# Mixer of a Fourier and FFN layer: four w_mod sums on GpSimd and ScalarE, splits and norm steps in another order

## The chip, the cores and the metric

The kernel runs on one core of one Trainium2 chip. TensorE does matrix products into PSUM, VectorE (DVE in the rows) and ScalarE (ACT) elementwise work, GpSimd (POOL) elementwise work in SBUF and some DMA issues, SyncE (SP) the other DMA issues. The metric is device time in microseconds (us) of one execution, smaller is better.

## The reference, cut to what matters

One layer (`DEPTH = 1`, so mixer 0) on 1024 tokens of width 1024, all in fp32:

```python
sh1, sc1, gt1, sh2, sc2, gt2 = ada_params(c, w_mod[i], b_mod[i])   # silu(c) @ w_mod + b_mod, six rows of 1024
a_lat = modulate(h_lat, g_norm_mix[i], sh1, sc1)                   # rms_norm(h, g) * (1 + scale) + shift
y_lat = fourier_mix(a_lat, w_fnet_out[j])                          # real part of a 2-D FFT, 4 groups of 256, then @ w_out
h_lat = h_lat + gt1 * y_lat
h_lat = h_lat + gt2 * conv_ffn(modulate(h_lat, g_norm_ffn[i], sh2, sc2), ...)
return rms_norm(h_lat, g_final)
```

`conv_ffn` is an up-projection to 2 x 2816 columns, a depthwise convolution over three tokens, silu times value, and a down-projection.

## The kernel before, in words

Products of fp32 are made of three reduced products: each operand is split into a high part (a cast on ScalarE) and a low part (a subtraction on VectorE). Such subtractions are called lows here.

**Stages.** The mixer takes the first 160 us or so. Two transforms (products with cosine and sine tables, lines 290 to 313 and 405 to 452) give the tiles `ph, pl, qh, ql` of four groups g, and the Nyquist row `p1`. Then `fnet_block(0)` multiplies them with the output weights `W` for the even tokens and `fnet_block(1)` for the odd ones, each in eight tiles dt of 128 channels; one dt is 25 matmuls (13 into `pw`, 12 into `qw`). ScalarE and VectorE put them into `ha`, GpSimd issues a DMA that adds x to it (line 555). Then each tile is squared (ScalarE, line 471), the squares are added (line 476), TensorE sums them over channels (`rstd_col`, tile `ssps`), VectorE and GpSimd make the inverse root (`r`, with a power on GpSimd), VectorE spreads it on a diagonal, and TensorE broadcasts it (`rb`). `norm2` multiplies by it and gives the operands of the FFN. The FFN begins with plain products `c<chunk><row><block>` (`plain`), and goes on in a seven-product scheme (X, Y, Z, then dX, dY), which is most of the run.

**w_mod.** The rows of `mods` are sums over a tile of w_mod (128 x 1024) times silu(c), one tile (s, n) for each of eight columns n: s = 2 is the gate gt1, 4 the FFN scale, 3 the FFN shift. `mod_sum` (line 145) does product and sum in one VectorE instruction; its second operand `silp` lies in PSUM. `silc` holds the same in SBUF. Each sum lets the next tile load (`wm_ahead`).

**Weights.** `w_prep` loads a unit k of the output weights, GpSimd makes sum and difference, ScalarE the high part; `w_lo(k)` is the low on VectorE, which also starts the load of unit k + 8; `w_last` does the same for the Nyquist weights `wl`.

**What sets the order.** Each engine works its instructions in order. VectorE's and SyncE's order is the order of the code from the start (`manual_schedule`), GpSimd's and ScalarE's from `fnet_block(0)` on, TensorE's from `fnet_block(1)` on; before these places a scheduler sets it. PSUM banks come from a ring of six (`bank`), so a product waits until the sixth tile before it has been read; two more are given by `small`, once `silp` is released (`after_sil`). The list `between` says what VectorE does between the groups of the second transform, `while_even` and `while_odd` what follows each dt, `amid_odd` what TensorE does between `pw` and `qw` of a dt.

## Time and profile before

| what | us |
|---|---|
| median of 3 runs | 825.66 |
| lowest, highest | 824.72, 827.84 |
| the profiled execution, its own time | 826.69 |
| its span, first to last instruction | 824.9 |
| TensorE busy | 778.9 |
| VectorE busy | 606.7 |
| ScalarE busy | 344.4 |
| GpSimd busy | 128.2 |

The rows further down come from the one profiled execution; its times count from the start of the span. "Busy" of TensorE does not say at which clock it ran: the granted clock is a column of its own.

### The profile page before, as it was taken

Reading aid. Unit: us, or ns where it says so; the run is one execution under the profiler, and the core shown is the slowest. Engines: PE = TensorE matmul, PEld = TensorE weight load, DVE = VectorE, ACT = ScalarE, POOL = GpSimd, SP = SyncE. Lnnn points to the kernel's source line nnn. Section 1 sums busy time; section 2 is a strip of 40 time slices with the busy share of each in tenths; the row PEclk is TensorE's granted clock in tenths of the full one; section 3 lists DMA queues with packets and bytes.
Section 4 is the critical chain, followed back from the end, with each engine's and each line's share of the span. In section 5 each row is a group of like instructions: output and inputs, shape, how many; then the busy total and the mean of one; then the engine's idle time right before and its main releaser. Section 6 shows DMA issues by size and latency. Waiting matters only on the chain.

```text
span 824.9 us, 10510 instructions
## 1 busy us (share of the span) xinstructions
PE 778.9 (94%) x3588; PEld 633.3 (77%) x3588; DVE 606.7 (74%) x1001; ACT 344.4 (42%) x617; POOL 128.2 (16%) x168
## 2 busy tenths in 40 slices
PE   1998979799999999999999999999999999999994
PEld 0585978588888888888888888888888888888883
DVE  5998976697867777877777777776747766648573
ACT  7364425425623334343333334433544435345520
POOL 2053431100112121212121121212110000000000
PEclk9999989799999999999999999999999999999995
DMA  9999764702398777858597778676999765655532
GB/s 331 407 335 341 217 178 91 217 27 89 89 288 204 199 192 205 242 142 246 146 254 198 193 221 256 141 195 155 266 294 356 231 191 184 199 183 176 182 149 102
DMA packets 81959, 171.30 MB, mean 208 GB/s; under 512 B 9001, under 2 KB 13865, under 8 KB 81906
## 3 DMA queue, kind: packets, MB, share of 16 engines
q1 hardware_dynamic: 67218, 143.89, 49.6%
q0 software_dynamic: 14688, 26.75, 20.4%
q8 instruction: 28, 0.46, 0.2%
q14 instruction: 25, 0.20, 0.1%
HBM read 130.49 MB, written 51.64 MB: 221 GB/s over the span
## 4 chain that ended last, share of the span: by engine, by line
PE 82%; DVE 9%; DMA 3%; issue 2%; ACT 2%; POOL 1%; POOLq 0%; DVEq 0%; SPq 0%; ACTq 0%
PE Y L693 19%; PE dX L1091 15%; PE X L693 13%; PE Z L693 13%; PE dY L1091 11%; PE c L693 8%; DVE wm L145 2%; DMA ha<-in_xt 2%; DMA wm<-in_wmod 1%; DVE ha L542 1%; PE ssps L1065 1%; DVE ha L572 1%; DVE z L216 1%; PE s2p L441 1%; DVE w L216 1%
## 5 line engine op out<-in xcount | busy, mean ns | idle before, releaser
L616 DVE TENSOR_TENSOR dn<-wd,dn 128x512 fp32r<-128x512 f32 x154 | 99.9, 689 | 69.3 <-ACT dn L612 68.6
L612 ACT CAST dn<-wd 128x512 fp32r<-128x512 f32 x154 | 88.6, 618 | 99.8 <-PE dX L1091 41.5
L1091 PE MATMUL dX<-dn,dn 128*128 128x512 f32 x528 | 123.5, 394 | 0.0
L1091 PEld LDWEIGHTS dX<-dn,dn 128*128 128x128 f32 x528 | 99.1, 188 | 23.2 <-issue 0.5
L755 POOL DMA_DIRECT2D ha<-ha x44 | 38.9, 968 | 348.2 <-DVE ha L696 158.7
L1091 PE MATMUL dY<-dn,dn 128*128 128x512 f32 x396 | 92.1, 394 | 0.0
L1091 PEld LDWEIGHTS dY<-dn,dn 128*128 128x128 f32 x396 | 74.4, 188 | 17.2
L696 DVE TENSOR_TENSOR ha<-Y,ha 128x512 f32<-128x512 f32 x57 | 39.4, 690 | 25.6 <-PE Y L693 25.6
L979 ACT COPY ha<-X 128x512 f32<-128x512 f32 x19 | 11.1, 586 | 110.2 <-PE X L693 110.2
L742 ACT ACTIVATE ha<-ha 128x512 f32<-128x512 f32 x44 | 27.8, 632 | 57.2 <-DVE ha L697 57.2
L145 DVE CUSTOM_DVE_ANT_0 wm<-wm,silp 128x1024 f32<-128x1024 f32 x32 | 37.9, 1213 | 0.4 <-DMA wm<-in_wmod 0.2
L1069 POOL TENSOR_TENSOR r<-r,mhalf 128x4 f32<-128x4 f32 x2 | 2.0, 1020 | 200.6 <-DVE r L1068 200.6
L798 POOL DMA_DIRECT2D sg_s<-in_wdn x22 | 29.9, 1373 | 9.2 <-DMA sg_s<-in_wdn 9.2
L798 POOL DMA_DIRECT2D sg_s<-sg_s x22 | 27.5, 1258 | 16.8 <-DMA sg_s<-sg_s 9.8
L697 DVE SCALAR_TENSOR_TENSOR ha<-ha,vec 128x512 f32<-128x512 f32 (+1 forms) x38 | 28.6, 752 | 1.4
L697 DVE SCALAR_TENSOR_TENSOR ha<-X,vec,ha 128x512 f32<-128x512 f32 (+1 forms) x38 | 28.4, 746 | 0.7
L696 DVE TENSOR_TENSOR ha<-Z,ha 128x512 f32<-128x512 f32 x38 | 26.0, 685 | 1.2 <-PE Z L693 1.2
L166 PE MATMUL gr<-wm,sil 128*32 128x512 f32 x32 | 10.3, 771 | 15.2 <-ACT sil L256 15.1
L696 DVE TENSOR_TENSOR ha<-ha 128x512 f32<-128x512 f32 x33 | 22.4, 685 | 0.0
L771 ACT COPY ha<-ha 128x512 f32<-128x512 f32 x11 | 6.8, 621 | 33.7 <-DVE ha L697 33.7
L166 PEld LDWEIGHTS gr<-wm,sil 128*32 128x32 f32 x32 | 3.1, 131 | 23.0 <-issue 20.6
L555 POOL DMA_DIRECT2D ha<-in_xt x14 | 12.7, 927 | 43.4 <-DVE ha L542 37.5
(947 smaller groups left out, 2000.2 us busy)
## 6 DMA issues: line engine op xcount, KB each, us to landing
wm<-in_wmod SPq DMA_DIRECT2D x40, 512.0 KB, 7.5
ha<-ha POOLq DMA_DIRECT2D x44, 256.0 KB, 5.2
sg_s<-in_wdn SPq DMA_DIRECT2D x44, 256.0 KB, 6.0
wd<-sg_s SPq DMA_DIRECT2D x44, 256.0 KB, 2.7
us_u<-ha SPq DMA_DIRECT2D x33, 256.0 KB, 2.0
wd<-in_wdn SPq DMA_DIRECT2D x33, 256.0 KB, 3.1
wd<-us_u SPq DMA_DIRECT2D x33, 256.0 KB, 3.4
us_T<-ha SPq DMA_DIRECT2D x22, 256.0 KB, 5.2
```

The costliest lines, as they stand in the source:

```text
L145: nc.vector.tensor_tensor_reduce(out=t, in0=t, in1=silp, scale=1.0, scalar=0.0, op0=ALU.mult, op1=ALU.add, accum_out=mods[:, s, n:n + 1])
L166: nc.tensor.matmul(rows[x][32 * j:32 * j + 32, :], lhsT=sil32[:, 4 * q + j, :], rhs=tiles[j][:, 512 * x:512 * x + 512], start=(q == 0), st ...
L216: nc.vector.scalar_tensor_tensor(out=t, in0=xraw[4 * i + f + 1][:, cs_], scalar=rr[:, 4 * i + f + 1:4 * i + f + 2], in1=xraw[4 * i + f][:, ...
L612: nc.scalar.copy(out=t[:, HALF[0]], in_=src)
L616: eng.tensor_tensor(out=t[:, HALF[1]], in0=src, in1=t[:, HALF[0]].bitcast(F32), op=ALU.subtract)
L693: nc.tensor.matmul(ps, lhsT=lh, rhs=rh, start=(first and j == 0 and x == 0), stop=(last and j == 3 and x == 2), skip_group_check=more)
L696: tt = lambda out, a, b, op, eng=nc.vector: eng.tensor_tensor(out=out, in0=a, in1=b, op=op)
L697: stt = lambda out, a, s, b, op0, op1: nc.vector.scalar_tensor_tensor(out=out, in0=a, scalar=s, in1=b, op0=op0, op1=op1)
L742: nc.scalar.activation(out=u[c, blk], in_=u[c, blk], func=AF.Silu)
L755: nc.gpsimd.dma_start(out=t, in_=other, accum_op=ALU.add)
L798: nc.gpsimd.dma_start(out=sg[n][k], in_=sg[a][k] if a[0] == "s" else block(k, a), accum_op=ALU.add, max_dma_last_dim=2048)
L1091: nc.tensor.matmul(BANKS[i][g], lhsT=lh, rhs=rh, start=(i in FIRST and k == 0 and x == 0), stop=(k == K2 - 1 and x == 2), skip_group_check ...
```

## The change

Four w_mod tiles, (4,1), (4,3), (3,2) and (3,4), are no longer summed by VectorE: GpSimd multiplies the tile by `silc` in place (`mod_mul`), and ScalarE adds it up with a copy that accumulates (`mod_acc`). In the second transform the two `p1` steps come ahead of the first weight lows, the lows are dealt out anew over `between`, and three w_mod sums come later in it. The even half's rms chain moves from dt 1 to dt 2 of the odd block; its first norm follows at the end of dt 2 (`late`), the last two w_mod sums of s = 3 stand inside the chain, and `ssps` takes a bank of the ring. Norms and up-projection lows of the first chunk come earlier in the odd block, its squares later. The odd half's chain moves from the first two products of the FFN into the third.

```diff
+    def mod_mul(s, n):
+        t = w_tiles.pop((s, n))
+        nc.gpsimd.tensor_tensor(out=t, in0=t, in1=silc, op=ALU.mult)
+        return s, n, t
+    def mod_acc(s, n, t):
+        nc.scalar.activation(out=t, in_=t, func=AF.Copy, accum_out=mods[:, s, n:n + 1])
+        wm_ahead(1)
...
     mod_tiles(2, 0, 8)
-    mod_tiles(4, 0, 4)
+    for n in (0, 2):
+        m = mod_mul(4, n + 1)
+        mod_tiles(4, n, n + 1)
+        mod_acc(*m)
...
-    w_lo(0, 1, 2, 3)
-    w_last(0)
     for ps, n, c0 in ((l0, 258, 0), (l1, 256, 258)):
...
+    w_lo(0, 1)
...
-    between = [lambda: (w_lo(4, 5), mod_tiles(4, 4, 5)), lambda: (w_lo(6, 7), w_last(1), mod_tiles(4, 5, 6)),
-               lambda: (gate1(), mod_tiles(4, 6, 8)),
-               lambda: (w_lo(8, 9, 10, 11), gate_ffn(), mod_tiles(3, 0, 1))]
+    between = [lambda: (w_lo(2, 3), w_last(0), w_lo(4)), lambda: (mod_tiles(4, 4, 5), w_lo(5, 6, 7), w_last(1)),
+               lambda: (gate1(), mod_tiles(4, 5, 7)),
+               lambda: (mod_tiles(4, 7, 8), w_lo(8, 9, 10, 11), gate_ffn(), mod_tiles(3, 0, 1))]
...
     def while_even(dt):
-        if dt:
-            mod_tiles(3, dt, dt + 1)
-        for d in {2: (0,), 3: (1,), 4: (2,), 5: (3,), 6: (4, 6), 7: (5, 7)}.get(dt, ()):
+        if dt in (1, 3):
+            later.append(mod_mul(3, dt + 1))
+        if dt in (1, 3, 4):
+            mod_tiles(3, {1: 1, 3: 3, 4: 5}[dt], {1: 2, 3: 4, 4: 6}[dt])
+        if dt in (2, 4):
+            mod_acc(*later.pop())
+        for d in {2: (0,), 3: (1,), 4: (2,), 5: (3,), 6: (4,), 7: (6, 5, 7)}.get(dt, ()):
...
     def while_odd(dt):
-        if dt > 2:
-            squares(1, dt - 3)
-            spill(1, dt - 3)
-            stat(1, dt - 3)
-        if dt == 0:
-            mod_bias(3, mods[:, 3, :])
-            after_sil()
-            load_raw(0, "g")
-            load_raw(0, "v")
-        elif 1 < dt < 6:
-            norm2(0, even[1], {2: (1, 2), 3: (3, 4), 4: (5, 6), 5: (7,)}[dt])
-            if dt == 3:
-                for n in ("A11", "A12", "A21", "A22"):
-                    ops[0, n] = op_hi(part(0, n), f"op0{n}")
-        if dt > 5:
-            for n in (("A11", "A12"), ("A21", "A22"))[dt - 6]:
-                op_lo(ops[0, n], part(0, n))
+        if 2 < dt < 6:
+            norm2(0, even[1], {3: (1, 2), 4: (3, 4, 5), 5: (6, 7)}[dt])
+        if dt == 5:
+            for n in ("A11", "A12", "A21", "A22"):
+                ops[0, n] = op_hi(part(0, n), f"op0{n}")
+            op_lo(ops[0, "A11"], part(0, "A11"))
+            op_lo(ops[0, "A12"], part(0, "A12"))
+        if dt > 5:
+            stats_odd(*{6: (0, 1, 2), 7: (3, 4)}[dt])
+        if dt == 7:
+            op_lo(ops[0, "A21"], part(0, "A21"))
+            op_lo(ops[0, "A22"], part(0, "A22"))
     def amid_odd(dt):
-        if dt == 1:
-            even.append(rstd_col(sacc[0], 512))
-            tb.append(stage("tb"))
-            rstd_diag(even[0], 512, tb[0][:, 512:])
-        elif dt == 2:
-            even.append(rstd_row(512, tb[0][:, 512:]))
+        if dt == 2:
+            even.append(rstd_col(sacc[0], 512, bank))
+            after_sil()
+            mod_tiles(3, 6, 7, silc)
+            tb.append(t_tile())
+            rstd_diag(even[0], 512, tb[0])
+            mod_tiles(3, 7, 8, silc)
+            mod_bias(3, mods[:, 3, :])
+            load_raw(0, "g")
+            load_raw(0, "v")
+    def late_odd(dt):
+        if dt == 2:
+            even.append(rstd_row(512, tb[0]))
             norm2(0, even[1], (0,))
...
+    def rms_odd():
+        C["rc"], C["dg"] = rstd_col(sacc[1], 512), t_tile()
+        rstd_diag(C["rc"], 512, C["dg"])
     plain(0, 1, 1, bank)
-    rc = rstd_col(sacc[1], 512)
-    dg1 = t_tile()
-    rstd_diag(rc, 512, dg1)
-    plain(0, 2, 1, bank, lambda: C.update(rb=rstd_row(512, dg1)))
+    plain(0, 2, 1, bank)
...
-    norm2(1, C["rb"], range(2))
...
-    plain(1, 1, 1, bank)
+    plain(1, 1, 1, bank, {("1", 0): rms_odd, ("2", 1): lambda: C.update(rb=rstd_row(512, C["dg"]))})
+    norm2(1, C["rb"], range(2))
```

On VectorE, in the second transform, before: the sums of w_mod tiles (4,2) and (4,3) (`wm_569`, `wm_572`), lows of units 0 to 3, then the `p` steps (`p1`), then the first split.

```order
L145 ISA wm_569,mods<-wm_569,silp 128x1024
...
L145 ISA wm_572,mods<-wm_572,silp 128x1024
...
L366 TENSOR_TENSOR w0l<-u_503,w0h 128x2x256
L366 TENSOR_TENSOR w1l<-u_509,w1h 128x2x256
L366 TENSOR_TENSOR w2l<-u_515,w2h 128x2x256
L366 TENSOR_TENSOR w3l<-u_521,w3h 128x2x256
L382 SCALAR_TENSOR_TENSOR wl<-wlh_666,vec,wlt_551 128x256
L422 SCALAR_TENSOR_TENSOR p_611<-p1h_671,vec,s2l_612 128x258
L422 SCALAR_TENSOR_TENSOR p_611<-p1h_674,vec,s2l_613 128x256
L403 TENSOR_TENSOR pl_599<-s2p_0_677,ph_595 128x258
```

The same place now:

```order
L145 ISA wm_569,mods<-wm_569,silp 128x1024
...
L433 SCALAR_TENSOR_TENSOR p_613<-p1h_640,vec,s2l_614 128x258
L433 SCALAR_TENSOR_TENSOR p_613<-p1h_643,vec,s2l_615 128x256
L376 TENSOR_TENSOR w0l<-u_503,w0h 128x2x256
L376 TENSOR_TENSOR w1l<-u_509,w1h 128x2x256
L416 TENSOR_TENSOR pl_601<-s2p_0_660,ph_597 128x258
```

The `p` steps moved ahead of all lows, and the sum of (4,3) has left VectorE's queue.

On GpSimd, in the even block, before: the DMAs that add x to `ha` and the additions of squares (`sacc`).

```order
L555 DMA ha<-in_xt 128x512 x4
L476 TENSOR_TENSOR sacc_828<-sacc_828,sq 128x512
L555 DMA ha<-in_xt 128x512
L476 TENSOR_TENSOR sacc_828<-sacc_828,sq 128x512
L555 DMA ha<-in_xt 128x512
L476 TENSOR_TENSOR sacc_828<-sacc_828,sq 128x512 x2
L555 DMA ha<-in_xt 128x512
L489 TENSOR_TENSOR r<-r,mhalf 128x4
```

The same place now (`wm_595` is tile (3,2), `wm_769` is (3,4)):

```order
L572 DMA ha<-in_xt 128x512 x2
L158 TENSOR_TENSOR wm_595<-wm_595,silc 128x1024
L572 DMA ha<-in_xt 128x512 x2
L158 TENSOR_TENSOR wm_769<-wm_769,silc 128x1024
L489 TENSOR_TENSOR sacc_830<-sacc_830,sq 128x512
L572 DMA ha<-in_xt 128x512
L489 TENSOR_TENSOR sacc_830<-sacc_830,sq 128x512
L572 DMA ha<-in_xt 128x512
L489 TENSOR_TENSOR sacc_830<-sacc_830,sq 128x512 x2
L572 DMA ha<-in_xt 128x512 x2
L505 TENSOR_TENSOR r<-r,mhalf 128x4
```

Two products came in among the DMAs, and two DMAs instead of one stand ahead of the power for `r`.

On ScalarE, in the second transform, now: the two accumulating copies (`wm_566` is tile (4,1), `wm_572` is (4,3)) among the copies of the first group.

```order
L432 CAST p1h_640<-s2l_614 128x258
L415 CAST ph_597<-s2p_0_660 128x258
L162 ACTIVATE wm_566,mods<-wm_566 128x1024
L415 CAST ph_597<-s2p_0_661 128x256
L432 CAST p1h_643<-s2l_615 128x256
L415 CAST qh_605<-s2q_662 128x512
L162 ACTIVATE wm_572,mods<-wm_572 128x1024
L415 CAST ph_598<-s2p_1_703 128x258
```

The copies were there before, without the two accumulating ones, and the second `p1h` stood behind the first `ph` of the next group.

## Rows read from the trace of the kernel before

**Rows 1.** The page, part 1: busy time of each engine, share, instructions.

```profile
PE 778.9 (94%) x3588; PEld 633.3 (77%) x3588; DVE 606.7 (74%) x1001; ACT 344.4 (42%) x617; POOL 128.2 (16%) x168
```

**Rows 2.** Waits of TensorE, whole span: total us, times, longest.

```profile
PE ssps L485 <- DVE sacc L476: 6.7, 2, 5.1
PE c L693 <- DVE op0A L616: 4.7, 1, 4.7
```

**Rows 3.** Three stretches: busy time of the engines, mean clock, DMA.

```profile
65.00:75.00 10.00, 7.50 (x27) 5.06 (x25) 9.54 (x21) 2.29 (x5) 0.06 (x1) 0.83 1.00 381
115.00:125.00 10.00, 7.64 (x36) 7.35 (x36) 4.97 (x14) 1.94 (x5) 2.82 (x3) 0.66 0.65 186
140.00:165.00 25.00, 17.95 (x72) 13.88 (x71) 16.77 (x33) 10.91 (x21) 3.62 (x4) 0.80 0.68 190
```

**Rows 4.** Timeline, second transform: start, duration (us), instruction, wait before it.

```profile
63.91 1.22 DVE L145 CUSTOM_DVE_ANT_0 wm<-wm,silp 128x1024 f32<-128x1024 f32 x1
...
70.04 0.48 DVE L422 SCALAR_TENSOR_TENSOR p<-p1h,vec,s2l 128x256 fp32r<-128x256 f32 x1 [0.44 <-ACT p1h L421]
...
69.65 2.08 PE L441 MATMUL s2p<-ac,dg 128*128 128x256 f32 x4 [2.50 <-DVE p L422]
```

**Rows 5.** Timeline of ScalarE, first stage: a square with its accumulator.

```profile
8.38 1.04 ACT L196 ACTIVATE junk<-xr 128x1024 f32<-128x1024 f32 x1
9.32 0.19 ACT L196 ACTIVATION_READ_ACCUMULATOR junk<-xr 128x1 f32 x1
```

**Rows 6.** Lines L358, L476 (duration ns least, median, most); two timeline rows.

```profile
L358 POOL TENSOR_TENSOR u<-u x16: 722/738/1174, 49.7 to 86.4; 128x256 f32<-128x256 f32 x16
...
L476 POOL TENSOR_TENSOR sacc<-sacc,sq x4: 1282/1612/1848, 101.5 to 111.2; 128x512 f32<-128x512 f32 x4
...
101.45 1.62 POOL L476 TENSOR_TENSOR sacc<-sacc,sq 128x512 f32<-128x512 f32 x1
...
101.50 2.13 DVE L366 TENSOR_TENSOR w3l<-u,w3h 128x512 fp32r<-128x512 f32 x1
```

**Rows 7.** Timeline: GpSimd on weight unit 8; TensorE at the first Fourier product.

```profile
76.76 1.17 POOL L358 TENSOR_TENSOR u<-u 128x256 f32<-128x256 f32 x1
...
82.58 0.36 PE L533 MATMUL pw<-ph,w0h 128*128 128x258 f32 x1 [0.74 <-ACT qh L402]
```

**Rows 8.** Chain of waits (start, us), end of the even half; one VectorE timeline row.

```profile
110.42 0.64 ACT sq L471
...
111.19 1.29 POOL sacc L476
...
117.36 1.87 PE ssps L485 x8
...
120.58 0.87 DVE L494 TENSOR_SCALAR tb<-ident,r 128x128 f32<-128x128 f32 x4 [1.16 <-POOL r L489]
```

**Rows 9.** Timeline, odd block: first norm, VectorE's wait for casts, first lows.

```profile
125.38 0.75 DVE L572 SCALAR_TENSOR_TENSOR ha<-ha,G,rb 128x512 f32<-128x512 f32 x1 [2.41 <-PE rb L499]
...
137.38 0.48 DVE L542 SCALAR_TENSOR_TENSOR ha<-qw,ngt,ha 128x256 f32<-128x256 f32 x1 [2.58 <-ACT ha L550]
...
147.16 1.29 DVE L616 TENSOR_TENSOR op0A<-wr0g,op0A 128x512 fp32r<-128x512 f32 x2
```

**Rows 10.** Chain of waits, FFN start (two rows); then timeline rows there.

```profile
149.53 5.27 DMA ha<-in_xt
...
162.70 58.25 PE c L693 x252
...
162.74 1.41 DVE L572 SCALAR_TENSOR_TENSOR ha<-ha,G,rb 128x512 f32<-128x512 f32 x2 [1.91 <-PE rb L499]
...
189.07 2.50 DVE L696 TENSOR_TENSOR T2l<-ha,T2h 128x512 fp32r<-128x512 f32 x4 [3.59 <-ACT T2h L714]
...
193.90 2.98 DVE L697 SCALAR_TENSOR_TENSOR ha<-c,vec,ha 128x512 f32<-128x512 f32 x4
...
198.62 0.39 PE L693 MATMUL c<-a2h,op2A 128*128 128x512 f32 x1
```

More of the change, by code (lines that the diff above doesn't have):

```diff
@@ L478, in fourier_ffn_kernel, with t_tile, rstd_col @@
     t2 = lambda: tmp.tile([P, 512], F32, tag="t2", bufs=2, name="sq")
-    def rstd_col(acc, n):
+    def t_tile():
+        return tmp.tile([P, 512], F32, tag="t2", bufs=2, name="t")
+    def rstd_col(acc, n, new=small):
         q = n // P
-        ps = small("ssps")
+        ps = new("ssps")
         for j in range(q):
@@ L517, in squares, with fnet_block @@
         ssq[blk, dt] = square(sacc[blk], ha[:, dt, 512 * blk:512 * blk + 512], dt, 512, t2)
-    def fnet_block(blk, then, mid=lambda dt: None):
+    def fnet_block(blk, then, mid=lambda dt: None, late=lambda dt: None):
         n = 258 if blk == 0 else 256
@@ L537, in fnet_block @@
                     mid(dt)
+            late(dt)
             gp, gn = mods[:, 2, dt:dt + 1], ngt1[:, dt:dt + 1]
@@ L592, in while_even @@
             stat(0, d)
+    later = []
     fnet_block(0, while_even)
@@ L686, in fourier_ffn_kernel, with product @@
     te, to = ([ha[:, dt, o:o + 512] for dt in range(KT)] for o in (0, 512))
-    def product(t, b, ps, first, last, more=False):
+    def product(t, b, ps, first, last, more=False, amid={}):
         for j in range(4):
+            amid.get((b[1], j), lambda: None)()
             hi, lo = t[:, j * P:(j + 1) * P], t[:, 512 + j * P:512 + (j + 1) * P]
@@ L820, in fourier_ffn_kernel, with plain @@
     load_raw(1, "v")
-    for dt in (5, 6, 7):
-        squares(1, dt)
-        spill(1, dt)
-        stat(1, dt)
+    stats_odd(5, 6, 7)
     C = {}
-    def plain(c, row, b, new, between=lambda: None):
+    def plain(c, row, b, new, amid={}):
         ps = C[c, row, b] = new(f"c{c}{row}{b}")
-        product(ops[c, f"A{row}1"], f"b1{b}", ps, True, False)
-        between()
-        product(ops[c, f"A{row}2"], f"b2{b}", ps, False, True)
+        product(ops[c, f"A{row}1"], f"b1{b}", ps, True, False, amid=amid)
+        product(ops[c, f"A{row}2"], f"b2{b}", ps, False, True, amid=amid)
     def gate_plain(c):
```

29 lines of the change are left out of this document (16 added, 13 removed).

## The prediction

> **What bounds the kernel now.** I read the page first. TensorE is busy for 94% of the span [rows 1], so time can be won only where it stands still or is clocked down. The waits of TensorE, longest first, say where [rows 2]: 6.7 us for the sums of squares (5.1 in the even half, 1.6 in the odd one) and 4.7 us for the first weight low of the up-projection. The timeline adds 2.5 us in the second transform, for the Nyquist row `p1` [rows 4]. All lie between 67 and 157 us; behind them TensorE runs without a gap to the last product. The view by stretches adds the other half of the price: around each of these waits the mean granted clock is below 1 [rows 3]. It has two levels, 2.4 and 1.2 GHz, and a mean of 0.66 says that two thirds of those 10 us ran at the lower. The share missing, times the stretch, is 1.7 us in the first, 3.4 in the second and 5.0 in the third, of which 1.5 fell on idle time: 8.6 us. Waits and clock together are some 23 us, the ceiling of any edit in this stretch.
>
> The timelines of VectorE, ScalarE and GpSimd show who is late. It is each time VectorE's queue, which works in the order written: a wait behind w_mod sums of 1.22 us each [rows 4], behind lows of weights, or behind its own long chain of norms. So the question is by how much VectorE's queue reaches its four urgent points earlier, and what is late next.
>
> **The second transform.** Before, VectorE reached `p1` after the sums of w_mod tiles (4,1), (4,2), (4,3), four lows and `wl`: the second of the two `p1` steps ran at 70.04, the first before it [rows 4]. Now they follow the sum of (4,2), which ends 1.15 us after 63.91: the first at 65.1. The second waits for its copy on ScalarE, which now stands behind the ScalarE sum of (4,1). That sum is priced by the two rows of the same shape, 1.04 + 0.19 us [rows 5]. The GpSimd product before it has no row of 128x1024. Its neighbours are 128x256 at 0.73 and 128x512 at 1.28 when undisturbed, 1.17 and 1.85 at worst [rows 6]; 0.55 us for each further 256 columns gives 2.4 us, four times the worst short one gives 4.7. I take 2.4, since the undisturbed rows lie on one line, and keep 4.7 for the range. The tile (4,1) has landed by 62.7, so product and sum end near 65.1 and 66.3, and the second `p1` runs at 66.9. TensorE wants the first freed bank at 67.15, where its wait began [rows 4], and the second at 68.1: the 2.5 us wait goes, with it the half clock behind it (1.7), and the last transform matmul ends at 77.6, 4.2 us earlier than the 81.8 of before [rows 7].
>
> Not all of that reaches the Fourier product. Its first bank is freed by the third split, which now stands on VectorE behind the second `wl`. That needs ScalarE's `wlh`, now behind the cast of weight unit 8 and the last `qh`. Unit 8 comes from GpSimd no earlier than before, at 77.9 [rows 7], because the load queue is full either way: two w_mod loads ahead of it on SyncE now wait for ScalarE's sums near 66 and 69, still 5 us before GpSimd began on that unit. Cast, `qh`, `wlh`, `wl` and split then give 80.4, against 82.6 before [rows 7]. **Gain so far 2.2 us**, and TensorE idles 2.8 us there; a half clock after it would cost 1.7, but the next wait (the fourth split, behind two w_mod sums in both orders, near 84.9) hides most of that.
>
> **The even half and its sums of squares.** Two products, (3,2) and (3,4), stand on GpSimd among the DMAs that add x, and two sums on ScalarE among the squares. What they do to VectorE is shown by one pair of rows: GpSimd's add began at 101.45 for 1.62 us, VectorE's low with both inputs in SBUF began at 101.50 and took 2.13 instead of 0.69 [rows 6]; it ended 0.56 after the add. I therefore let the low that meets a product end after it: 1.3 us lost at (3,2), 2.6 at (3,4), which cancels the lead won so far: the sum of (3,3) starts at 103.5 as before. From there VectorE has two w_mod sums left instead of five, 3.4 us less. The end is then set elsewhere: GpSimd's add of the fifth square tile still ends at 112.5 [rows 8], since its DMA is issued no earlier; two squares of 0.6 and two adds of 0.6 remain. The sums are ready at **114.8 instead of 117.3** [rows 8]. TensorE, which now does 25 more products (3.0 us) before it wants them, arrives near 114. So the column sums start at 114.9, with 3.0 us more work behind TensorE: 5.5 us ahead, and the 5.1 us wait shrinks to about 1.
>
> The chain to the broadcast: before, column sums started at 117.36 and the diagonal was ready at 121.45 [rows 8]. Now the power on GpSimd stands behind two DMA issues of 0.88 instead of one, and VectorE updates two tiles instead of one before it; the column sums at full clock save 0.9. The w_mod sum put between r and the diagonal lies beside the power. The diagonal is ready at 119.5, and since only 12 matmuls (1.4 us) stand between, TensorE waits 0.7 to 2.2 us, which is new. The next w_mod sum delays the first norm to 120.8, against 125.38 [rows 9].
>
> **Norms and first product.** From that norm to the first lows of the up-projection VectorE took 125.38 to 147.16 [rows 9]. In between lay 2.6 us of waiting for ScalarE, which made four casts of the up-projection first [rows 9], three adds of squares and one pair of updates (2.9), all of which now come later; 21.8 less 5.5 is 16.3, and 0.4 for the changed turns with ScalarE. The two weight loads of that chunk now issue after the chain instead of at the odd block's start, behind the same spills on SyncE; they are wanted 16 us later, over twice what a load takes here, so they cost nothing unless those spills are late. Lows start at 137.5 and the first is there at 138.2; TensorE, free near 135.5 to 137, waits until then. Before, the first low was there at 147.85 [rows 9]. **Gain 9.7 us.**
>
> **Odd half.** The product matmul takes 0.231 us (252 in 58.25 [rows 10]). The first product ends at 143.3; the second waits 0.8 us for its low, now behind two updates and four adds, and ends at 149.75. The odd sums: the last update at 142.7, its DMA 5.27 [rows 10], square and add 1.3, so 149.4. Column sums start at 149.75, where before they came after one product, and the half clock, at 156.4; the second product was still to come. TensorE alone would now be 14.1 us ahead: the column sums, the broadcast and 144 matmuls need 34.8 us, so it would want c211 at 184.5.
>
> But VectorE gets the odd broadcast later in TensorE's order (15 matmuls into the third product): its norms begin 5.5 us after the column sums, at 155.2. Before, from 162.74 to the end of the convolution that frees the bank of c211, 196.88, it took 34.1 us, of which 3.6 were a wait for ScalarE [rows 10]; 30.5 without it. That bank is free at 185.7, and TensorE stands 1.2 us. c211 started at 198.62 [rows 10]: **12.9 us** earlier. Behind it VectorE has its own waits again and TensorE is the bound to the end, so the lead stays.
>
> The profiled execution took 826.69 us, 1.0 above the median 825.66: 826.69 - 12.9 = 813.8. I say 814.0.
>
> **Rivals.** (1) The clock gives part back: new waits of 2.8 (before the Fourier product), 1 to 2 (broadcast) and 1 to 2.5 us (first product) each put TensorE at half clock, 1.7 lost each as in the first stretch of rows 3, and twice it falls on TensorE's own path: 3 to 6 us. For it: 1.6 us of idle before the odd column sums was followed by the lower level [rows 2, 3]. Against: between them VectorE, not TensorE, sets the pace. 817 to 820.
>
> (2) The lock: every product holds VectorE for its whole length, not only the two that I counted. Four times 2.4 is 9.6, of which 3.9 are in the sum: 5.7 more, 819.5; at 4.7 for a product beyond 821. For it: the 2.13 us low [rows 6]. Against: the first two products meet w_mod sums and `p1`, whose second input is in PSUM. The Trainium skill (SBUF - State Buffer, Who interferes with whom) states that a VectorE instruction with two SBUF inputs and a GpSimd instruction that reads SBUF exclude each other for the whole instruction; this trace agrees, with that low of 2.13. The Trainium skill (GPSIMD Engine Reference, Performance versus the Vector engine) gives 4497 ns for a two-input fp32 add of 2048 columns; an estimate from that page is 2.25 us for a product, and the sum, in which two products lie on the path, would be 813.5.
>
> (3) Slower. Each microsecond x by which a product is dearer than 2.4 shifts (3,2) and then (3,4), behind which DMA issues, squares and the third and fourth late lows queue: the sums come 2x later, and nothing hides it. The 12.9 are used up at x = 6.5, a product of 8.9 us; 10 us give 829. Nothing in rows 6 comes near.
>
> (4) The change shifts waits only: the last DMAs land as before, or VectorE's norms, no longer held by TensorE, are held by ScalarE, and under 4 us remain: 823 to 827.
>
> (5) More: no low meets a product, so that the sums are ready by 113.5, and the odd chain follows: 809 to 811.
>
> **How the numbers follow.** Forecast 0.50, (1) 0.22, (2) 0.08, (3) 0.04, (4) 0.07, (5) 0.09. The forecast's own range is 811 to 817. The range 808.5 to 821.0 takes in (1), most of (5) and half of (2), and leaves out under 0.2. A measurement of this kernel can tell 0.5%, 4.1 us, from no change. Faster by more: forecast, (1), (5) and most of (2), 0.88; same 0.08; slower 0.04.
>
> **What would show it.** Right: no wait at the second transform's `p1`; the Fourier product from about 80; column sums of the even half near 115, of the odd half near 150, the latter without a wait; c211 near 186; products of 2.4 us. Wrong: products over 4 us, half clock after 80 or in the first product, or TensorE waiting at c211 for more than 3 us.

## The result, and the profile after

The changed kernel takes 815.21 us (median of 4 runs, 814.38 to 817.29); the kernel before took 825.63 beside it. The ratio is 0.9866, interval 0.984 to 0.9893: 10.4 us faster by the two medians, 11.1 by the ratio, and 1.2 us above the forecast of 814.0. Its profiled execution took 815.39 us, 11.3 less than that of before (826.69).

First the page of the kernel after, two of its parts: busy time by engine, and the granted clock of TensorE in 40 slices of the span, in tenths.

```profile
PE 773.4 (95%) x3588; PEld 628.1 (77%) x3588; DVE 606.7 (75%) x993; ACT 348.7 (43%) x625; POOL 138.1 (17%) x172
...
PEclk9999899999999999999999999999999999999996
```

Then TensorE's waits of the kernel after (waited for: total, times, longest), to be laid beside [rows 2]. Three lines are left out, because before they were there as well, at about the same size: 15.8 us in the first stage, and two of 2.3 us, one for a load in the first stage, one at the last norm.

```profile
PE pw L549 <- DVE pl L416: 3.7, 1, 3.7
...
PE rb L515 <- DVE t L510: 1.7, 1, 1.7
PE c L725 <- ACT op0A L634: 1.6, 1, 1.6
PE c L725 <- DVE op0A L638: 1.1, 2, 1.0
PE qw L549 <- DVE ha L559: 1.1, 1, 1.1
```

The 6.7 us for the sums of squares are gone, and of the 4.7 us at the first weight low 0.15 remain (in the timeline below; the other 1.0 of that line is the low of the second product). `p1` is gone too. New are 3.7 us in front of the Fourier product, 1.7 for the broadcast and 1.1 for a `ha` of VectorE, and the wait for ScalarE's cast at the first product grew from 0.7 to 1.6.

The view by stretches of the kernel after (stretch, length, busy time of PE, PEld, DVE, ACT, POOL, mean granted clock, DMA), to be laid beside [rows 3]; the second line is a stretch that ran at full clock before.

```profile
65.00:75.00 10.00, 10.00 (x40) 6.54 (x39) 8.76 (x17) 5.72 (x14) 3.33 (x2) 1.00 1.00 380
80.00:90.00 10.00, 8.00 (x46) 8.03 (x47) 9.31 (x18) 4.35 (x10) 8.35 (x12) 0.66 0.70 228
115.00:125.00 10.00, 8.34 (x65) 7.66 (x64) 7.81 (x18) 3.56 (x8) 2.82 (x3) 1.00 0.98 269
140.00:165.00 25.00, 23.43 (x101) 18.00 (x102) 17.83 (x35) 12.24 (x23) 2.77 (x3) 1.00 0.56 179
```

The three stretches that ran at 0.83, 0.66 and 0.80 of full clock [rows 3] are at 1.00; one new stretch, 80 to 90, is at 0.66. It comes right behind the new wait: TensorE stands from 78.3 to 82.0 and then runs at the lower of its two levels, 1.2 GHz.

Last, TensorE's marks along the span (timeline of the kernel after: start, duration, instruction, wait before it): column sums and broadcast of the even half, the first product's first use of a weight low, column sums of the odd half, c211.

```profile
118.02 0.95 PE L501 MATMUL ssps<-ones,sacc 128*128 128x1 f32 x8
...
122.16 1.12 PE L515 MATMUL rb<-t,ones 128*128 128x512 f32 x2 [1.66 <-DVE t L510]
...
140.74 0.72 PE L725 MATMUL c<-a2h,op0A 128*128 128x512 f32 x2 [0.15 <-DVE op0A L638]
...
152.66 0.94 PE L501 MATMUL ssps<-ones,sacc 128*128 128x1 f32 x8
...
188.36 0.39 PE L725 MATMUL c<-a2h,op2A 128*128 128x512 f32 x1
```

Against before: the Fourier product starts 0.6 us earlier (82.00 against 82.58 [rows 7]). The even column sums start 0.7 later than before [rows 8], but with 25 more products behind TensorE and no wait. The first weight low is used at 140.74 instead of 147.90, so the lead is 7.2; c211 starts 10.3 us earlier than the 198.62 of before [rows 10], and the span ends 11.3 earlier. The last 1.0 us arises behind c211, and since the distance from c211 to the end lies between 624.2 and 626.3 us in the executions below, whatever was edited, I put it down to the spread of single executions.

### The profile page after: what moved, and what is told of

Same layout as the page of the kernel before. It is cut to its first block, busy times and chain, and to the rows that moved or that the text cites. A ratio compares the mean times of both kernels' runs of the same rounds, so it can differ in the third digit from the quotient of the medians.

```text
span 813.6 us, 10520 instructions
## 1 busy us (share of the span) xinstructions
PE 773.4 (95%) x3588; PEld 628.1 (77%) x3588; DVE 606.7 (75%) x993; ACT 348.7 (43%) x625; POOL 138.1 (17%) x172
## 4 chain that ended last, share of the span: by engine, by line
PE 81%; DVE 9%; DMA 3%; POOL 2%; issue 2%; ACT 2%; SPq 1%; POOLq 0%; DVEq 0%; ACTq 0%
PE Y L725 19%; PE dX L1117 15%; PE X L725 13%; PE Z L725 13%; PE dY L1117 11%; PE c L725 7%; DVE wm L145 2%; DMA xr<-in_xf 1%; DMA wm<-in_wmod 1%; DMA ha<-in_xt 1%; PE ssps L1091 1%; PE pw L549 1%; DVE ha L589 1%; DVE z L226 1%; POOL sacc L489 1%
## 5 line engine op out<-in xcount | busy, mean ns | idle before, releaser
L145 DVE CUSTOM_DVE_ANT_0 wm<-wm,silp 128x1024 f32<-128x1024 f32 x26 | 30.8, 1213 | 1.9 <-DMA wm<-in_wmod 1.8
L176 PE MATMUL gr<-wm,sil 128*32 128x512 f32 x32 | 10.5, 786 | 15.8 <-ACT sil L266 15.8
```

Of the source, the lines that this page charges most:

```text
L145: nc.vector.tensor_tensor_reduce(out=t, in0=t, in1=sil, scale=1.0, scalar=0.0, op0=ALU.mult, op1=ALU.add, accum_out=mods[:, s, n:n + 1])
L176: nc.tensor.matmul(rows[x][32 * j:32 * j + 32, :], lhsT=sil32[:, 4 * q + j, :], rhs=tiles[j][:, 512 * x:512 * x + 512], start=(q == 0), st ...
```

## The experiments

The prediction's total held, so the question was whether its parts did. The theory at this point: two things pay, the odd rms chain's place and VectorE's order between the norms and the first lows; the GpSimd products give back by the lock (VectorE and GpSimd holding each other up) what they spare. The rival is the prediction's own account, in which tiles and transform pay their share too. All runs in one table; each run is timed beside the kernel before on its chip, and the ratios compare best. Marks are those of one profiled execution, and such an execution can be off by itself: code that is the same up to the Fourier product gave 80.97, 83.45 and 85.38 there in three runs (last section). So the medians carry the verdicts, and the marks tell where the time went.

| run | median us | ratio to before (interval) | Fourier product | even column sums | c211 |
|---|---|---|---|---|---|
| before | 825.63 | | 82.58 | 117.36 | 198.62 |
| changed kernel | 815.21 | 0.9866 (0.984 to 0.9893) | 82.00 | 118.02 | 188.36 |
| e1_tiles_on_vector | 814.55 | 0.9862 (0.9817 to 0.9907) | 81.17 | 114.83 | 187.72 |
| e2_transform_order | 819.57 | 0.9935 (0.9896 to 0.9973) | 86.37 | 121.32 | 193.72 |
| e5_rms_only | 814.71 | 0.9876 (0.984 to 0.9912) | 80.97 | 114.50 | 187.39 |
| e6_tiles_only | 830.41 | 1.005 (1.0027 to 1.0073) | 87.62 | 124.27 | 203.52 |
| e3_even_chain_dt1 | 814.66 | 0.9856 (0.9803 to 0.9908) | 81.94 | 117.05 | 190.12 |
| e4_odd_chain_before | 820.77 | 0.9942 (0.9918 to 0.9966) | 80.94 | 117.57 | 193.78 |
| e7_adds_between_norms | 820.07 | 0.993 (0.9903 to 0.9957) | 83.45 | 116.71 | 194.25 |
| f3_casts_behind_splits | 817.12 | 0.9899 (0.9862 to 0.9936) | 80.11 | 120.50 | 190.85 |
| f31_casts_and_tiles | 814.66 | 0.9872 (0.9838 to 0.9905) | 79.24 | 114.43 | 187.38 |
| g1_issues_behind_power | 815.61 | 0.9871 (0.9845 to 0.9896) | 85.38 | 117.87 | 189.78 |
| g2_with_casts | 815.29 | 0.9866 (0.9842 to 0.9889) | 79.76 | 115.69 | 187.89 |
| g3_lock_and_casts | 810.68 | 0.9798 (0.9767 to 0.983) | 79.77 | 114.96 | 184.50 |

### The four tiles back on VectorE

```
-    for n in (0, 2):
-        m = mod_mul(4, n + 1)
-        mod_tiles(4, n, n + 1)
-        mod_acc(*m)
+    mod_tiles(4, 0, 4)
...
-        if dt in (1, 3):
-            later.append(mod_mul(3, dt + 1))
...
+        if 0 < dt < 5:
+            mod_tiles(3, dt, dt + 1 + (dt == 4))
```

> The changed kernel with its four w_mod tiles (4,1), (4,3), (3,2), (3,4) back on VectorE as sums of 1.21 us; every other move stays. Theory (lock): in the even half VectorE lost 1.6 us at one low (2.28 instead of 0.68) and 3.8 us at another (4.47) beside the two GpSimd products, more than the 2.4 us of sums that they spared it, so the sums of squares come 1 to 3 us earlier than 117.3; in front of the transform p1 comes 2 us later and TensorE waits about 2 us there, but the Fourier product still starts near 82, since it hangs on the cast of weight unit 8. Total 814 to 817, within 2 us of the changed kernel's 815.2. Rival (VectorE's queue is the bound and every sum taken off it counts): 4 x 1.21 = 4.9 us slower than the changed kernel, about 820.

814.55 us, as the theory had it: 4.9 us of sums went back onto VectorE and nothing became slower. The even column sums came 3.2 us earlier than in the changed kernel. The reason stands in the timelines of GpSimd and VectorE of the changed kernel, around the product on tile (3,4):

```profile
102.43 2.71 POOL L158 TENSOR_TENSOR wm<-wm,silc 128x1024 f32<-128x1024 f32 x1
104.79 1.60 POOL L489 TENSOR_TENSOR sacc<-sacc,sq 128x512 f32<-128x512 f32 x1
...
102.47 4.47 DVE L376 TENSOR_TENSOR w3l<-u,w3h 128x512 fp32r<-128x512 f32 x1
106.87 1.21 DVE L145 CUSTOM_DVE_ANT_0 wm<-wm,silp 128x1024 f32<-128x1024 f32 x1
```

A low of 0.68 us began 0.04 after the product and lasted 4.47, past the product and past the add that GpSimd had queued behind it. The product spared VectorE 1.2 us and cost it 3.8, of which some 1.5 would have gone to the add alone, as in [rows 6].

Only one part of the expectation missed: `p1` did not come 2 us later with four sums ahead of it (67.35 for the second step against 67.73), and TensorE's 2 us wait there did not appear. In this run the four sums follow each other without a wait. In the changed kernel VectorE, with two sums fewer, waits instead, for tile (4,2) to land and, at the second step, for its copy on ScalarE. Timeline of VectorE of the changed kernel:

```profile
64.86 1.22 DVE L145 CUSTOM_DVE_ANT_0 wm<-wm,silp 128x1024 f32<-128x1024 f32 x1 [1.30 <-DMA wm<-in_wmod]
...
67.73 0.48 DVE L433 SCALAR_TENSOR_TENSOR p<-p1h,vec,s2l 128x256 fp32r<-128x256 f32 x1 [1.24 <-ACT p1h L432]
```

Together the two waits, 2.5 us, are as long as the two sums that left.

### The order of the transform undone, with the tiles on GpSimd

```
-    w_lo(0, 1)
...
+    w_lo(0, 1, 2, 3)
+    w_last(0)
     for ps, n, c0 in ((l0, 258, 0), (l1, 256, 258)):
...
```

> The changed kernel with the order of the second transform on VectorE as before (four lows and wl ahead of p1, w_mod sums placed as before); the tiles on GpSimd and both rms chains stay as changed. Theory: p1 comes about 3 us later, TensorE waits some 2 us for its bank and runs at half clock behind it, the transform ends 3 us later (81 instead of 78.3), but the Fourier product starts only about 1 us later than 82.0, because in the changed kernel it waited 3.7 us for the third split behind the cast of weight unit 8 anyway. Total 816 to 817.5. Rival (the whole lead of the transform, 3 to 4 us, is passed on to the end): 818.5 to 820.

819.57: the theory missed and the rival's 4 us are there. But they are not what the new order gains over before. TensorE waited 4.0 us for `p1`, where before it waited 2.5 [rows 4]. The reason is in the timelines of GpSimd and VectorE of this run:

```profile
66.67 2.65 POOL L158 TENSOR_TENSOR wm<-wm,silc 128x1024 f32<-128x1024 f32 x1 [1.05 <-DVE w0l L376]
...
67.03 2.83 DVE L376 TENSOR_TENSOR w2l<-u,w2h 128x512 fp32r<-128x512 f32 x1
```

With the lows ahead of `p1`, one of them meets the product on tile (4,3) and is held for 2.83 us, and `p1` with it. So the new order of the transform is worth 4 us only where products stand on GpSimd.

### Neither tiles nor transform: the rms chains alone

This run takes both edits above back together. What is left of the change is the placement of chains, norms, casts and adds.

> Only the placement of the two rms chains and norms is left of the change: the four w_mod tiles are sums on VectorE, and the second transform has its order of before. Theory: the Fourier product starts as before (82.6), nothing on VectorE is held by a GpSimd product, so from there to the first product it takes 57.7 us as with the tiles on VectorE, and from there to c211 48.5 us: c211 near 188.8, total 815 to 816.5, all of the gain with neither the tiles nor the order of the transform. Rival (tiles and transform carry their share of the gain): 818 to 820.

814.71, the whole gain. The Fourier product came 1.6 us earlier than expected, which is not this edit's doing but the spread of single executions (last section). The marks of this run on TensorE's timeline:

```profile
80.97 0.36 PE L547 MATMUL pw<-ph,w0h 128*128 128x258 f32 x1 [0.79 <-DVE pl L413]
...
114.50 1.05 PE L499 MATMUL ssps<-ones,sacc 128*128 128x1 f32 x8 [0.25 <-DVE sacc L487]
...
187.39 0.39 PE L719 MATMUL c<-a2h,op2A 128*128 128x512 f32 x1
```

With the runs so far the table of two by two is full: tiles on VectorE 814.7 (old order) and 814.6 (new order); tiles on GpSimd 819.6 (old order) and 815.2 (new order). The tiles cost 4.9 us in the old order and at most 0.7 in the new one. The latter is less than the runs can tell. They gain in neither, and without them the new order gains nothing.

### The tiles alone, on the kernel before

> The kernel before with the four w_mod tiles alone on GpSimd and ScalarE; transform, chains and norms as before. Theory: the product on tile (4,3) meets one of the four weight lows ahead of p1 and holds it for its whole length (2.8 us instead of 0.7), p1 comes 1 to 2 us later than 69.1 and 70.0, the Fourier product near 85 to 86.4 instead of 82.6, and in the even half two more lows are held, so that VectorE wins nothing there: total 827 to 830, slower than before by 1.5 to 4. Rival (each sum off VectorE's queue counts): 821 to 824.

830.41, 0.5% slower (interval 0.27% to 0.73%), just past the upper end. `p1` came 3.6 us later where 1 to 2 was expected, and the Fourier product at 87.62 where 85 to 86.4 was. Timelines of VectorE and GpSimd:

```profile
66.63 1.22 DVE L145 CUSTOM_DVE_ANT_0 wm<-wm,silp 128x1024 f32<-128x1024 f32 x1 [2.87 <-DMA wm<-in_wmod]
...
68.38 2.83 DVE L376 TENSOR_TENSOR w1l<-u,w1h 128x512 fp32r<-128x512 f32 x1
...
72.74 0.47 DVE L435 SCALAR_TENSOR_TENSOR p<-p1h,vec,s2l 128x258 fp32r<-128x258 f32 x1
...
67.94 2.73 POOL L158 TENSOR_TENSOR wm<-wm,silc 128x1024 f32<-128x1024 f32 x1 [0.21 <-DVE mods L145]
```

Two things delay `p1` by 3.6 us against the first step of before (69.11): VectorE waits for tile (4,2) to land, and one low is held for 2.83. Why the tile lands later there was not tried.

### The even chain one tile earlier

```
-        if 2 < dt < 6:
-            norm2(0, even[1], {3: (1, 2), 4: (3, 4, 5), 5: (6, 7)}[dt])
+        if 1 < dt < 5:
+            norm2(0, even[1], {2: (1, 2), 3: (3, 4, 5), 4: (6, 7)}[dt])
...
-        if dt == 2:
+        if dt == 1:
             even.append(rstd_col(sacc[0], 512, bank))
```

> The changed kernel with the even rms chain (column sums, diagonal, broadcast, norms) one tile of the odd block earlier, as early as before: column sums in tile 1, 25 matmuls (3.0 us) sooner in TensorE's order. Theory: the sums are ready near 117 as in the changed kernel, TensorE is there at 115, waits 2.3 us and runs at half clock behind it; the norms start at most 1 us earlier, so the first product starts 1 to 2.5 us later than 139.9. Total 816 to 818. Rival (the place of the chain is worth the whole wait that went there, 5 us): 820 to 821. Second rival (the chain on VectorE sets the first product, TensorE's wait is free): 814 to 815.5.

814.66 in time, which is the second rival's; the profiled execution took 816.35, which is the theory's, and in it the first product started 2.0 us and c211 1.8 us later than in the changed kernel, as the theory had it. The four times lie between 813.57 and 816.35. So whether the place of the even chain costs up to 2 us or nothing stays open; it is worth nothing like 5 us. Timeline of TensorE in this run:

```profile
117.05 1.45 PE L501 MATMUL ssps<-ones,sacc 128*128 128x1 f32 x8 [2.41 <-DVE sacc L489]
...
121.69 2.07 PE L515 MATMUL rb<-t,ones 128*128 128x512 f32 x2 [0.42 <-DVE t L510]
```

The wait came back at the sums (2.4, as expected) and went elsewhere: 1.2 less at the broadcast, and the 1.6 for the cast of the first product is gone. So most of the wait moved from one place to another.

### The odd chain where it was

```
     plain(0, 1, 1, bank)
-    plain(0, 2, 1, bank)
+    rms_odd()
+    plain(0, 2, 1, bank, {("2", 0): lambda: C.update(rb=rstd_row(512, C["dg"]))})
...
+    norm2(1, C["rb"], range(2))
+    op_lo(ops[1, "A21"], part(1, "A21"))
+    op_lo(ops[1, "A22"], part(1, "A22"))
...
-    plain(1, 1, 1, bank, {("1", 0): rms_odd, ("2", 1): lambda: C.update(rb=rstd_row(512, C["dg"]))})
-    norm2(1, C["rb"], range(2))
-    op_lo(ops[1, "A21"], part(1, "A21"))
-    op_lo(ops[1, "A22"], part(1, "A22"))
+    plain(1, 1, 1, bank)
```

The first two norms of the odd half and two lows go back with the chain, ahead of four weight loads.

> The changed kernel with the odd rms chain where it was before: column sums behind the first product of the up-projection, broadcast in the middle of the second; all else as changed. Theory: the last add of squares ends near 150.9, TensorE wants the sums at 146.5, waits about 4 us and runs at half clock behind it, c211 starts 5 to 6 us later than 188.4: total 820 to 821. Rival (VectorE's norms set c211; they start 1.7 us earlier, so TensorE's wait is made up for): 813.5 to 815.5.

820.77, inside the theory's range. Timeline of TensorE in this run:

```profile
150.90 1.87 PE L501 MATMUL ssps<-ones,sacc 128*128 128x1 f32 x8 [5.29 <-DVE sacc L489]
...
193.78 0.39 PE L725 MATMUL c<-a2h,op2A 128*128 128x512 f32 x1
```

TensorE, now early, reaches the odd sums 5.3 us before they are there (about 4 expected), and the column sums themselves run at the lower clock (1.87 instead of 0.94). c211 is 5.4 us later than in the changed kernel. By the medians that is 5.6 us, about half of the gain.

### Adds and casts between the norms

On the run with the rms placement alone, the adds of squares start again in tile 3 and the four casts stand in tile 4, ahead of the last norms; the lows follow from tile 6. Which of the three costs what was not tried apart.

```
+        if dt > 2:
+            stats_odd(dt - 3)
...
+        if dt == 4:
+            for n in ("A11", "A12", "A21", "A22"):
+                ops[0, n] = op_hi(part(0, n), f"op0{n}")
```

> The run with only the rms placement, with one thing of it taken back: the squares and adds of the odd half start again three tiles behind (one in each turn from tile 3 on) and the four casts of the up-projection stand in tile 4, between the norms; the lows follow from tile 6. The chains keep their places. Theory: VectorE's way from the first norm to the first low grows by three adds, a pair of updates and waits for ScalarE, 4 to 5.5 us, TensorE waits that much longer in the first product, about half of it comes back since the odd sums are then ready sooner than needed: total 817 to 820 against 814.7. Rival (VectorE's order between norms and lows has slack, only the two chains' places count): 814 to 815.5.

820.07, 5.4 above the run it was made from. Timeline of TensorE in this run:

```profile
146.56 1.22 PE L720 MATMUL c<-a2h,op0A 128*128 128x512 f32 x2 [6.02 <-DVE op0A L632]
...
194.25 0.39 PE L720 MATMUL c<-a2h,op2A 128*128 128x512 f32 x1
```

6.0 us of waiting for the first low, where the run it was made from waits 1.65 for a cast. From the even column sums to c211 it is 77.5 us instead of 72.9, so what the theory let come back did not. (The even column sums too are 2.2 later than in that run, behind the late Fourier product of this execution.)

With the 5.6 us of the odd chain (820.77 less 815.21) the two edits cost 11.0 us by the medians, against a gain of 10.4; by the ratios 10.7 against 11.1. So these two edits account for the whole gain. Each was undone by itself, from a different kernel, and not both together; the smaller parts of the placement (the bank of `ssps`, the time of the weight loads, the order of the even squares) were not tried apart.

### Casts of weight units behind the splits

In the changed kernel ScalarE stood with its queue behind GpSimd's unit 8, in front of the last `qh` and `wlh`. Timelines of ScalarE and TensorE of the changed kernel:

```profile
79.21 0.62 ACT L369 CAST w0h<-u 128x512 fp32r<-128x512 f32 x1 [2.21 <-POOL u L368]
79.73 0.58 ACT L415 CAST qh<-s2q 128x512 fp32r<-128x512 f32 x1
80.21 0.41 ACT L391 CAST wlh<-wlt 128x256 fp32r<-128x256 f32 x1
...
82.00 0.55 PE L549 MATMUL pw<-ph,w0h 128*128 128x258 f32 x1 [3.69 <-DVE pl L416]
```

Two runs put the casts of units 8 to 15 behind the last split (ScalarE and GpSimd in written order from there on) and VectorE's gate vectors and two sums behind the fourth split; the second also has the four tiles on VectorE.

```
-        nc.scalar.copy(out=W[g][0][:, :, qs], in_=u[:, 0:2])
+        if k < 8:
+            w_mix(k)
+            w_cast(k)
...
+               lambda: (),
+               lambda: ([w_mix(k) for k in range(8, 16)], w_cast(8, 9, 10, 11, 12), gate1(), mod_tiles(4, 5, 8),
```

> The changed kernel with the casts of weight units 8 to 15 on ScalarE behind the last split of the transform, and the gate vectors and two w_mod sums on VectorE behind the fourth split. Theory: the 3.7 us wait in front of the Fourier product came from ScalarE's cast of unit 8 ahead of qh and wlh; without it the product starts near 79.5 instead of 82.0 and the half clock behind the wait (6.8 us, 3.4 lost, partly beside waits) shrinks; the lead reaches c211 as far as VectorE follows: total 811 to 813.5. Rival (VectorE's queue up to the sums of squares sets the pace; TensorE waits there instead): 814.5 to 816.

> The same with the four w_mod tiles back on VectorE as sums. Theory: no product holds a low, the sums of squares are ready 2 to 3 us earlier than with the products, and TensorE has the lead to use it: total 809.5 to 812.5, under the run with the products on GpSimd by 0.5 to 2. Rival (with TensorE earlier, the 4.9 us of sums are missing on VectorE after all): 1 to 3 us above that run.

817.12 and 814.66. The two lie 2.5 us apart, a little more than expected, but their intervals overlap. The wait in front of the Fourier product shrank to 1.5 and 1.3 us, as expected, and brought nothing: the first theory missed by 3.6 us, the second by 2.2. With the tiles on VectorE the column sums start at 114.43, and in the run without this edit (tiles on VectorE, new order of the transform) at 114.83, though the Fourier product started 1.9 us apart. VectorE's queue between 84 and 114 has a single wait of over a microsecond in either run, so a Fourier product earlier than 81 gains nothing there: VectorE, not TensorE, sets the even sums.

With the products on GpSimd the sums of squares are ready at 117.3, as in the changed kernel, but TensorE arrives only at 120.50. Being early, it waits 1.68 us for the low that met the product on tile (3,4), which lasted 4.45 us here and 4.47 in the changed kernel. The next wait, 1.07 for `ha`, is the same in both, and they leave it at 108.76 and 108.93. Then only this run drops to half clock: timeline of TensorE in this run, and the stretch behind in both (this run, then the changed kernel).

```profile
106.83 0.39 PE L561 MATMUL pw<-ph,w3l 128*128 128x258 f32 x1 [1.68 <-DVE w3l L386]
...
108.00:118.00 10.00, 9.24 (x55) 9.24 (x56) 8.52 (x19) 3.43 (x7) 5.62 (x5) 0.66 0.72 194
...
108.00:118.00 10.00, 9.07 (x75) 9.08 (x76) 8.73 (x22) 4.09 (x9) 5.68 (x5) 1.00 0.70 181
```

The 2.5 us are that stretch: 55 matmuls began in it against 75, and c211 is 2.5 us later as well.

### A version that is faster than both

The remaining waits all lay on VectorE's way from the even sums to the first low. A first try started from the run with the rms placement alone. It put GpSimd's two DMA issues behind the power, tile 2's update ahead of the first norm, two norms in each tile, the four casts in tile 4 and the odd squares in tile 7. A second added the new order of the transform and the casts behind the splits.

> The run with only the rms placement, with VectorE's path behind the even sums shortened: the two DMA issues of the odd block's first tiles stand on GpSimd behind the power, the update of tile 2 stands ahead of the first norm on ScalarE and VectorE, norms follow two to a tile, and the squares of the odd half wait until tile 7. Theory: the power is ready 0.9 to 1.7 us sooner, TensorE's 2.2 us wait for the broadcast shrinks to about 1, VectorE's 3.0 us of waits between the first norm and the first low go, the first product starts 2 to 3.5 us earlier (near 135.5 instead of 138.6) and c211 with it: total 811 to 813. Rival (the odd sums, whose last DMA lands no sooner, take TensorE's lead back at the end of the second product): 814 to 815.

> The same with the casts of weight units 8 to 15 behind the last split of the transform and the gate vectors and two sums behind the fourth split. Theory: the Fourier product starts near 79.3 instead of 81, but the sums of squares are set by VectorE and the last DMAs (ready at 114.4 in both runs seen so far), so it gains nothing over the run without it: within 0.7 us of it. Rival (with the later part shortened, the earlier lead counts): 1 to 2 us faster.

815.61 and 815.29: no gain, and the theory of the first missed by 2.6 us and more; the second stood to the first as expected. (In its profiled execution the first reached the Fourier product 4.4 us later than the run it was made from, at the same code up to there, so all its marks are late.) Timelines of GpSimd and VectorE of the first show two faults:

```profile
119.10 1.95 POOL L503 TENSOR_TENSOR r<-r,mhalf 128x4 f32<-128x4 f32 x1 [4.32 <-DVE r L501]
...
118.93 1.22 DVE L145 CUSTOM_DVE_ANT_0 wm<-wm,silc 128x1024 f32<-128x1024 f32 x1
...
136.65 0.48 DVE L559 SCALAR_TENSOR_TENSOR ha<-qw,ngt,ha 128x256 f32<-128x256 f32 x1 [2.57 <-ACT ha L567]
```

The power now stands behind no DMA issue, but beside VectorE's w_mod sum, whose inputs both lie in SBUF, and takes 1.95 us; and the four casts, which I had put into tile 4, hold VectorE for 2.57 as they did before [rows 9]. The last run mends both and moves a few more things:

```
-            even.append(rstd_col(sacc[0], 512, bank))
-            after_sil()
-            mod_tiles(3, 6, 7, silc)
+            mod_tiles(3, 6, 7, silc)
+            even.append(rstd_col(sacc[0], 512, bank))
+            after_sil()
...
+        if dt == 5:
+            for n in ("A11", "A12"):
+                ops[0, n] = op_hi(part(0, n), f"op0{n}")
+            norm2(0, even[1], (6, 7))
+            for n in ("A21", "A22"):
+                ops[0, n] = op_hi(part(0, n), f"op0{n}")
```

> The run before it (casts behind the splits, issues behind the power, tile 2's update ahead of the first norm) with its two faults mended and three more waits aimed at: the w_mod sum that held GpSimd's power (1.95 us beside the sum, 1.03 alone) stands ahead of the column sums' result, and the updates of the odd block's first two tiles behind it; the casts of the up-projection stand in tile 5, two ahead of the last norms and two behind; the second wl stands behind the last split; the first two squares of the even half stand one tile later, and three unit casts behind the update of tile 1. Theory: the power starts behind nothing and is ready 0.9 us sooner, VectorE's waits between norms and lows (2.6 us at one place) go, the first low comes 19.6 us after the column sums instead of 23 to 24, TensorE starts the first product near 135 and c211 near 184.5 to 186 instead of 187.4 to 187.9: total 810 to 812.5. Rival (the odd sums or VectorE's later norms take the lead back by c211): 814 to 815.5.

810.68 us, as the theory had it, and c211 at 184.50 too; its interval lies wholly below that of the changed kernel. Timelines of GpSimd, VectorE and TensorE:

```profile
116.19 1.03 POOL L514 TENSOR_TENSOR r<-r,mhalf 128x4 f32<-128x4 f32 x1 [5.32 <-DVE r L512]
...
117.26 0.90 DVE L519 TENSOR_SCALAR t<-ident,r 128x128 f32<-128x128 f32 x4 [0.36 <-POOL r L514]
...
135.83 1.28 DVE L650 TENSOR_TENSOR op0A<-wr0g,op0A 128x512 fp32r<-128x512 f32 x2
...
136.56 0.76 PE L741 MATMUL c<-a2h,op0A 128*128 128x512 f32 x2 [1.82 <-DVE op0A L650]
...
184.50 0.39 PE L741 MATMUL c<-a2h,op2A 128*128 128x512 f32 x1
```

From column sums to diagonal it is 2.3 us instead of 3.2, and VectorE has no wait over 0.5 us between the first norm and the first low, which runs 20.9 us behind the column sums instead of 22.0 (19.6 expected). Not all of what was moved was tried apart.

## Why the prediction was right, and where it was not

**The second transform: mechanism right, gain not.** TensorE's 2.5 us wait for `p1` and the half clock behind it went as said. The two steps of `p1` ran at 66.00 and 67.73 (said: 65.1 and 66.9), the transform ended at 78.3 (77.6). What failed is the step "Unit 8 comes from GpSimd no earlier than before, at 77.9", from which 80.4 was made. Its reason, that the loads are issued "still 5 us before GpSimd began on that unit", left out that they take about that long to land (a median of 4.7 us from issue to landing in the kernel after). Unit 8's loads stand on SyncE behind a w_mod load, which now waits for ScalarE's second sum, and they went out 3.3 us later than before. Timelines of SyncE of the kernel after (first two lines) and before, and of GpSimd of the kernel after:

```profile
69.92 0.33 SPq L132 DMA_DIRECT2D wm<-in_wmod  x1
70.34 0.38 SPq L365 DMA_DIRECT2D u<-in_wfa  x1
...
67.03 0.33 SPq L355 DMA_DIRECT2D u<-in_wfa  x1
...
78.01 1.17 POOL L368 TENSOR_TENSOR u<-u 128x256 f32<-128x256 f32 x1
```

GpSimd began its round at 76.05 instead of 74.94 and finished unit 8 at 79.2; with the tiles on VectorE, where the loads went out at 68.49, it was 78.35. Cast, `qh`, `wlh`, `wl` and split followed from there: 82.0, a gain of 0.6 instead of 2.2. The first rival priced what came next. After 3.7 us of standing TensorE ran at half clock: its matmuls start 0.21 us apart until 87.5, and 0.12 behind that. That the Fourier product matters little was right as well, but for another reason: with it at 81.17 or 79.24 the even sums came at 114.83 or 114.43 (tiles on VectorE), so VectorE sets them. In the runs with a later one they came later as well: 116.71 behind 83.45, 117.87 behind 85.38.

**The lock: under-sized, and the tiles' share wrong.** The products took 2.36 to 3.08 us (2.4 said), and ScalarE's sums 1.06 and 0.19. I let each low that meets a product end a little after the product, so that the sum of (3,3) would start at 103.5. The first lost 1.6 us (1.3 said). The second began 1.0 us later than the same low before (102.47 against 101.50 [rows 6]), so there was no lead to cancel, and it also waited out the add behind the product: it lost 3.8 (2.6 said), and the sum of (3,3) started at 106.87. The sums of squares were ready at 117.3 instead of 114.8, where they had been before; in the same kernel with the tiles on VectorE they are ready at 114.8. So the step "From there VectorE has two w_mod sums left instead of five, 3.4 us less" took for a gain what the same products had already cost.

The second rival had the mechanism, though not in every product: the first two cost VectorE only 0.45 us, at one low. It cost little in time because the late sums are mostly made up behind them. With the tiles on VectorE the column sums start 3.2 us earlier but the first lows only 1.0 (139.00 against 140.00): TensorE then waits 2.25 us for the broadcast and makes it at half clock, 2.07 us instead of 1.12. The Trainium skill (SBUF - State Buffer, Who interferes with whom) has a VectorE instruction with two SBUF inputs and a GpSimd instruction that reads SBUF exclude each other for the whole instruction. The runs agree both ways round, with 4.47 us for a low that takes 0.68 elsewhere and 1.95 for a power that takes 1.03 beside other work.

**The chain and the norms: right.** TensorE's wait for the broadcast was said to be 0.7 to 2.2 and was 1.66. From the first norm (123.39) to the first lows (140.00) it took 16.6 us (16.7 said), and undoing that order alone, on the kernel with only the rms placement, cost 5.4. The place of the even chain itself, one tile later, is worth 2 us at most. The lead at the first low was 7.2 instead of 9.7, because the first norm came at 123.39 instead of 120.8; all of that stood already at the even sums, 118.02 instead of 114.9.

**The odd half: right.** The second product's wait was 0.98 (0.8 said). The odd column sums ran without a wait at 152.66, 2.9 later than said, about as late as everything ahead of them. c211 followed 35.7 us behind them (35.95 said), and undoing the chain's place cost 5.6. The 1.2 us of standing at c211 did not show as a wait of TensorE.

**The sum.** 12.9 were said to c211, 10.3 came, and 1.0 more behind it in that execution. That the odd chain's place and VectorE's order behind the even norms pay was right, and these two account for the whole gain. That the total came within 1.2 us of the forecast is in part luck: the sum also held the tiles and the transform to be gains, and these are one cost of 4.9 us (tiles in the old order) and one repair of 4.4 (the new order with the tiles in place), which cancel.

## What to carry to other kernels

Before an operation goes to another engine to relieve a queue, look at what its new neighbour does to the queue: lows with two SBUF inputs on VectorE beside GpSimd's products cost here at least as much as the sums that left (0 to 4.9 us net, by the order). A chain that several engines share is best placed where its consumer arrives anyway, and on the engine that sets the pace nothing that is wanted later may stand ahead of what is wanted now: these two moves gave 10 us, and the last version, which went on in the same way, 4.5 more. And undo each part of a change by itself and in pairs, since a part that mends what another part broke looks like a gain.

## What the runs showed of the hardware

- A VectorE low that met GpSimd did not get its turn between two GpSimd instructions: 4.47 us across a product of 2.71 and an add of 1.60, 4.45 in another run. Where only a product stood there, lows took 2.83 beside 2.65 and 2.73.
- The exclusion works the other way as well: the power of 128x4 took 1.95 us beside VectorE's w_mod sum with both inputs in SBUF, and 1.03 beside updates one of whose inputs lies in PSUM.
- The same instructions reach the Fourier product at different times in different executions: with identical code up to there, 80.97, 83.45 and 85.38 in three runs. They part at `p1`. TensorE waited 2.46, 2.51 and 3.16 us for it, and from 65 to 75 its mean granted clock was then 1.00, 0.83 and 0.76 of full. So nearly the same wait (2.46 and 2.51) was followed by full clock once and by the lower level once; what decides it isn't shown. Timelines of TensorE, the same four matmuls behind the wait in the first run and in the second:

```profile
70.43 1.96 PE L452 MATMUL s2q<-ac,dg 128*128 128x512 f32 x4
...
70.80 3.58 PE L452 MATMUL s2q<-ac,dg 128*128 128x512 f32 x4
```
